# Silu and tanh gates in the input projections, and the delta rule's stream first in the scan, in a hybrid encoder block

## Chip, cores and metric

One kernel computes one encoder block on one core of a Trainium2 chip. The metric is the device time of a run in microseconds; lower is better. The engines are TensorE (PE in the rows; PEld are its weight loads), VectorE (DVE), ScalarE (ACT), GpSimd (POOL), and SyncE (SP), whose queue issues most DMAs.

## What is computed

All arrays are fp32, 512 tokens (T), width 2048 (D). Cut to what matters here:

```python
h = rmsnorm(x); proj = h @ w_in                        # columns: q k v z beta/alpha | Q F B I g
q, k, v = silu(short_conv(q, k, v)); q, k = l2norm(q), l2norm(k)
o_a = gdn_scan(q, k, v, fwd) + gdn_scan(..., bwd)      # gated delta rule, 8 heads
y_a = rmsnorm(o_a) * silu(z)
f = lb + (1 - lb) * sigmoid(F or B)                    # forget gates, one per direction
o_b = hgrn_scan(silu(Q), I, 1 - f, log f) both ways    # 8 heads
y_b = rmsnorm(o_b) * sigmoid(g)
x = x + concat(y_a, y_b) @ w_out
x = x + (silu(h2 @ w_gate) * (h2 @ w_up)) @ w_down     # h2 = rmsnorm(x)
out = rmsnorm(x)
```

The table of lower bounds `lb` comes from a softmax over two rows of logits.

## The kernel before

The kernel is one instruction stream that a scheduler of the language puts in order: it follows the order in which the Python code emits instructions, as a priority, and lets ready work go ahead by its own timing model. Each engine then runs its own list strictly in order, and so does each DMA queue.

Every large matrix product is done by `block_products`, in blocks of 256 output columns, with seven products for eight (a Strassen-like scheme, `PRODUCTS`), each operand split in a high and a low part (three matmuls each). All its matmuls stand in one line, L1022. Weights come by DMA as `raw` (SP queue) and are turned into `wsum` (VectorE, L974 to L976), `whr` and `whs` (high parts, ScalarE, L981 and L985), `wls` (low part, VectorE, L986) and `wlr` (low part; in the projections, the output projection and the down projection ScalarE writes the negative high part, L980, and a DMA issued by GpSimd adds `raw` to it, L982).

The stages, in order of the profile's time:

**Projections** (to about 842 us). `projections` walks the list `AHEAD` of 36 blocks: `k`, `q`, `v`, `z` of the delta rule, and `Q`, `F`, `B`, `I`, `g` of HGRN2, 0 to 3 each; the last two, `B3` and `g2`, are done together. After a block `combine` and L423 give `t`, 128 x 1024, and `post` finishes it and stores it to DRAM. `sigmoid` (L319 to L324) is exp(-x), ln(1 + .), exp(-.), three ACTIVATEs into the tile `sig`, of which there is one buffer. For `k`, `q`, `v` `conv_silu` first makes the five-tap convolution `acc`, then multiplies by the sigmoid on GpSimd (L338); `z` and `Q` are multiplied in L396, also on GpSimd; `F` and `B` take VectorE's L390 with `lb`, `g` takes the sigmoid as it is. `q` and `k` are normalised in the middle of the next block: two Ln (L355) and an Exp (L357 or L359). In the later blocks (`PREP`, indices 18 to 27) `gdn_head` prepares decay matrices for a head, with Abs and Exp on ScalarE (L478, L479) and multiplies on GpSimd (L477, L489), and `gdn_inverse` inverts 32 x 32 blocks on VectorE.

**Scan** (to about 1115 us). `gdn_blocks` and `gdn_pair` handle two heads of the delta rule, in four dependent steps forward and backward at once; `hgrn_pair` handles two heads of HGRN2, in seven levels that double the width, where VectorE multiplies X in place (L748, L750), ScalarE copies `kc` (L719) and TensorE multiplies (L722, L738), and then three dependent steps. Each pair ends in `finish` (L438 to L452): Square (L441), a sum over the partitions on TensorE (L445), two Ln (L446), an Exp (L447), two multiplies (L448, L451) and a store to `d_y`; its tiles have one buffer each. `merge` interleaves the streams: each generator yields a nominal duration, and the stream that is furthest behind emits next. PSUM is split: `psh` and `poh` for the HGRN pairs, `pss` and `pog` for the delta rule.

**Output projection** (`out_proj`). `Y_BLOCKS` gives the order in which the heads' outputs are loaded from `d_y` and used: 0 and 2 are the halves of the delta rule, 4 and 6 those of HGRN2. PSUM is now four pools of two banks, `ps0` to `ps3`, in the place of `psh`, `pss`, `poh`, `pog`; `Banks.take` gives the first column block pools 0 and 2, the next pools 1 and 3, and so on in turn. The first two column blocks are interleaved.

**FFN** (`gate_up`, `down`), with Silu in L1065.

The set of ScalarE's functions is asked for by name at the start (L88, the set that holds Ln and Exp) and near the end (L1105). In the profile one more load stands at L1065, in front of the first Silu, which the code doesn't ask for.

Of the kernel before, what the change touches and what calls it, by code (L numbers as in the profile page):

```python
# [9 lines left out]
F32 = mybir.dt.float32  # L10
# [7 lines left out]
P = 128  # L18
T = 512
# [51 lines left out]
class Block:  # L71
# [51 lines left out]
    def small_columns(self, pt, tmp):  # L123

        nc, a, const = self.nc, self.a, self.const
        lev = tmp.tile([P, 2, T], F32, name="sq", bufs=1).rearrange("p a t -> p (a t)")[:, :len(LEVELS) * 32]
        lev = lev.rearrange("p (l t) -> p l t", t=32)
        nc.sync.dma_start(out=lev, in_=a["c_lev"])
        self.tc.keep_in_program_order(nc.gpsimd.tensor_copy(out=self.lev, in_=lev))
        nc.sync.dma_start(out=self.tri, in_=a["c_tri"])  # L130
        self.tc.keep_in_program_order(nc.gpsimd.tensor_copy(out=self.trim, in_=self.tri))
        r1, r2 = self.r1, self.r2
        nc.tensor.transpose(out=pt[:, 0:120], in_=r1, identity=self.ident[0:120, 0:120])
        nc.tensor.transpose(out=pt[:, 128:178], in_=r2, identity=self.ident[0:50, 0:50])
        self.convw = const.tile([P, 5, 24], F32, name="convw")
        nc.vector.tensor_copy(out=self.convw.rearrange("p k c -> p (k c)"), in_=pt[:, 0:120])
        self.cols = const.tile([P, 50], F32, name="cols")
        nc.vector.tensor_copy(out=self.cols, in_=pt[:, 128:178])
        self.w2 = self.cols[:, 32:48]
        self.wga, self.whb = self.cols[:, 48:49], self.cols[:, 49:50]  # L140

        l0, l1 = self.cols[:, 0:16], self.cols[:, 16:32]
        m = tmp.tile([P, 16], F32, name="lbm")
        e = tmp.tile([P, 2, 16], F32, name="lbe")
        nc.vector.tensor_tensor(out=m, in0=l0, in1=l1, op=ALU.max)
        nc.vector.tensor_tensor(out=e[:, 0], in0=l0, in1=m, op=ALU.subtract)
        nc.vector.tensor_tensor(out=e[:, 1], in0=l1, in1=m, op=ALU.subtract)
        nc.scalar.activation(out=e, in_=e, func=AF.Exp)
        nc.vector.tensor_tensor(out=m, in0=e[:, 0], in1=e[:, 1], op=ALU.add)
        nc.vector.reciprocal(out=m, in_=m)  # L150
        self.lb = const.tile([P, 2, 16], F32, name="lb")
        nc.vector.tensor_tensor(out=self.lb[:, 0], in0=e[:, 0], in1=m, op=ALU.mult)
        nc.vector.tensor_scalar(out=self.lb[:, 1], in0=self.lb[:, 0], scalar1=-1.0, scalar2=1.0, op0=ALU.mult, op1=ALU.add)

# [157 lines left out]
    def projections(self, xops, chunk, tmp):  # L314
# [1 line left out]
        w = a["w_in"][0]  # L316
        ht = self.HT

        def sigmoid(src):  # L319
            s = tmp.tile([P, 2, T], F32, name="sig", bufs=1)  # L320
            nc.scalar.activation(out=s, in_=src, func=AF.Exp, scale=-1.0)
            nc.scalar.activation(out=s, in_=s, func=AF.Ln, bias=1.0)
            nc.scalar.activation(out=s, in_=s, func=AF.Exp, scale=-1.0)
            return s  # L324

        def conv_silu(t, ct):
            acc = tmp.tile([P, 2, T], F32, name="acc", bufs=2)
            for kk in range(2):
                w_ = lambda j: self.convw[:, j, ct + kk:ct + kk + 1]
                nc.scalar.activation(out=acc[:, kk], in_=t[:, kk], func=AF.Copy, scale=w_(2))  # L330
                for j in (0, 1, 3, 4):
                    sh = j - 2
                    o = slice(max(0, -sh), T - max(0, sh))
                    i = slice(max(0, sh), T - max(0, -sh))
                    nc.vector.scalar_tensor_tensor(out=acc[:, kk, o], in0=t[:, kk, i], scalar=w_(j), in1=acc[:, kk, o],
                                                   op0=ALU.mult, op1=ALU.add)
            s = sigmoid(acc)
            nc.gpsimd.tensor_tensor(out=acc, in0=acc, in1=s, op=ALU.mult)  # L338
            return acc

        def qk(t, col, dst, bias):
            acc = conv_silu(t, col // P)
# [34 lines left out]
        def post(kind, g, t):  # L377
            if kind == "k":
                return qk(t, OFF_K + g * 256, self.d_k[g], None)
            if kind == "q":  # L380
                return qk(t, OFF_Q + g * 256, self.d_q[g], self.qbias)
            if kind == "v":
                return tokens(conv_silu(t, (OFF_V + g * 256) // P), self.d_v[g])
            if kind == "I":
                return tokens(t, self.d_hv[g])
            s = sigmoid(t)
            if kind in "FB":
                for kk in range(2):
                    r = (kind == "B") * 8 + 2 * g + kk
                    nc.vector.tensor_scalar(out=s[:, kk], in0=s[:, kk], scalar1=self.lb[:, 1, r:r + 1],  # L390
                                            scalar2=self.lb[:, 0, r:r + 1], op0=ALU.mult, op1=ALU.add)
                dst = self.d_hf[(kind == "B") * 4 + g]
            elif kind == "g":
                dst = self.d_g[H // 2 + g]
            else:
                nc.gpsimd.tensor_tensor(out=s, in0=s, in1=t, op=ALU.mult)  # L396
                dst = (self.d_g if kind == "z" else self.d_hq)[g]
            nc.scalar.dma_start(out=dst.rearrange("h p t -> p h t"), in_=s)

# [441 lines left out]
    def scan(self):  # L841
        tc = self.tc
        with ExitStack() as st:
            pool = lambda name, **k: st.enter_context(tc.tile_pool(name=name, reuse_waits="tile", **{"bufs": 1, "side": "right", **k}))
            for n, b in (("psh", 2), ("pss", 2), ("poh", 1), ("pog", 1)):
                setattr(self, n, st.enter_context(tc.tile_pool(name=n, bufs=b, space=PSUM, reuse_waits="tile")))
            first, second, rest = pool("sca"), pool("scb"), pool("scc")
            self.sca = Pools(rest, hf=first, hq=first, C=first, X=second)
            self.sch, self.fin = pool("sch"), pool("fin")
            self.scb = pool("sc1"), pool("sc2", side="left")  # L850
            self.sc = pool("sc")
            self.gdn_ready = {}

            def gdn():
                yield from self.gdn_blocks(0)
                for i in range(0, H, 2):
                    yield from self.merge((0, self.gdn_pair(i)), *([(0, self.gdn_blocks(i + 2))] if i + 2 < H else []))

            def faster(i):
                for dt in self.hgrn_pair(i):  # L860
                    yield 0.75 * dt

            for _ in self.merge((0, faster(0), faster(4)), (40, faster(2), faster(6)), (40, gdn())):
                pass


    Y_BLOCKS = (0, 4, 6, 2)
    Y_SLOTS = (6, 7, 0, 1, 2, 3, 4, 5)

    def out_proj(self, late):  # L870
# [318 lines left out]
```

## Time and profile before

| | |
|---|---|
| time, median of 3 runs | 2677.78 us (2677.45 to 2679.18) |
| time of the profiled execution | 2677.02 us |
| its span, first to last instruction | 2675.2 us |
| mean granted TensorE clock | 0.968 of full speed |
| busy: TensorE, VectorE, ScalarE, GpSimd | 93%, 86%, 56%, 19% |

Shares of the whole span mix stages with different limits; the rows below are therefore taken by stretch. A row of instructions names line, engine, operation, output <- inputs with their shapes, and the count; "idle before" is time in which the engine waited, with what ended the wait.

### The profile page before, as it was taken

What the parts mean: (1) busy time and instruction counts of PE and PEld (TensorE: products, weight loads), DVE (VectorE), ACT (ScalarE), POOL (GpSimd) and SP (SyncE); (2) the same over time, 40 slices, a digit from 0 to 9 for tenths busy, and PEclk for the clock granted to TensorE, in tenths of its full rate; (3) what the DMA queues carried; (4) which work ended last, traced back from release to release, by engine and by line L of the source; (5) the groups of instructions that cost most, each with busy time, mean ns of one, the idle gap of its engine ahead of it and who ended that gap; (6) DMA issues with size and microseconds to landing.
All of it is one profiled execution on the core that took longest, in us unless ns stands there. A gap on an engine that the chain in (4) does not pass through costs nothing.

```text
span 2675.2 us, 55501 instructions
## 1 busy us (share of the span) xinstructions
PE 2489.8 (93%) x22511; PEld 2437.7 (91%) x22511; DVE 2298.1 (86%) x3598; ACT 1497.4 (56%) x2057; POOL 519.9 (19%) x400
## 2 busy tenths in 40 slices
PE   7999999989997788799999999999999989998996
PEld 6999999889986667799899999999999989998996
DVE  7989989998976876877988989889889888888885
ACT  7787777666665433656644444444444455655664
POOL 1233224443333532222000000000000012222221
PEclk9999999999998888999999999999999999999998
DMA  8889999999897443799343344333333388887875
GB/s 228 191 200 210 212 204 223 232 220 239 200 233 201 108 122 113 220 243 251 118 135 127 123 123 126 122 116 121 125 114 123 121 250 196 213 190 178 195 157 142
DMA packets 401708, 465.71 MB, mean 174 GB/s; under 512 B 48449, under 2 KB 354043, under 8 KB 401451
## 3 DMA queue, kind: packets, MB, share of 16 engines
q1 hardware_dynamic: 310939, 311.67, 38.3%
q0 software_dynamic: 71936, 103.83, 24.2%
q10 hardware_dynamic: 18576, 46.67, 5.0%
q8 instruction: 176, 2.88, 0.4%
q14 instruction: 81, 0.66, 0.1%
HBM read 303.66 MB, written 54.62 MB: 134 GB/s over the span
## 4 chain that ended last, share of the span: by engine, by line
PE 67%; DMA 10%; DVE 9%; issue 7%; ACT 4%; POOL 1%; SPq 1%; ACTq 0%; DVEq 0%; POOLq 0%
PE big L1022 64%; DMA wlr<-raw 4%; DMA raw<-in_w_out 1%; DVE X L750 1%; DVE wls L986 1%; DVE X L748 1%; DMA acc<-d_rows 1%; DMA tt<-d_t 1%; DMA raw<-in_w_down 1%; ACT wlr L980 1%; ACT whs L985 0%; ACT whr L981 0%; DVE wsum L975 0%; DMA sl<-d_l 0%; DVE wsum L974 0%
## 5 line engine op out<-in xcount | busy, mean ns | idle before, releaser
L985 ACT CAST whs<-wsum 128x1024 fp32r<-128x1024 f32 (+1 forms) x448 | 461.8, 1033 | 470.2 <-PE big L1022 242.4
L986 DVE TENSOR_TENSOR wls<-wsum,whs 128x1024 fp32r<-128x1024 f32 (+1 forms) x448 | 563.2, 1258 | 151.4 <-ACT whs L985 146.7
L982 POOL DMA_DIRECT2D wlr<-raw x272 | 323.7, 1190 | 1889.1 <-DVE tsum L941 893.8
L1022 PE MATMUL big<-oh,whs 128*128 128x256 f32 x2368 | 661.8, 283 | 3.7 <-ACT whs L985 3.7
L1022 PE MATMUL big<-ol,whs 128*128 128x256 f32 x2368 | 661.4, 282 | 0.0
L1022 PE MATMUL big<-oh,wls 128*128 128x256 f32 x2368 | 646.4, 283 | 3.3 <-DVE wls L986 3.3
L1022 PE MATMUL big<-oh,wlr 128*128 128x256 f32 x1776 | 493.4, 282 | 23.0 <-DMA wlr<-raw 22.8
L1022 PE MATMUL big<-oh,whr 128*128 128x256 f32 x1776 | 499.4, 283 | 13.2 <-ACT oh L956 9.8
L1022 PE MATMUL big<-ol,whr 128*128 128x256 f32 x1776 | 496.7, 281 | 0.6 <-DVE ol L958 0.6
L1022 PEld LDWEIGHTS big<-oh,whs 128*128 128x128 f32 x2368 | 449.9, 190 | 5.0 <-ACT whs L985 5.0
L1022 PEld LDWEIGHTS big<-ol,whs 128*128 128x128 f32 x2368 | 450.4, 190 | 0.0
L1022 PEld LDWEIGHTS big<-oh,wls 128*128 128x128 f32 x2368 | 443.3, 191 | 4.4 <-DVE wls L986 3.9
L1022 PEld LDWEIGHTS big<-oh,wlr 128*128 128x128 f32 x1776 | 332.9, 189 | 26.8 <-DMA wlr<-raw 26.5
L1022 PEld LDWEIGHTS big<-oh,whr 128*128 128x128 f32 x1776 | 335.7, 189 | 17.5 <-ACT oh L956 12.6
L974 DVE TENSOR_TENSOR wsum<-raw 128x512 f32<-128x512 f32 (+1 forms) x448 | 314.5, 703 | 42.0 <-DMA raw<-in_w_out 20.2
L1022 PEld LDWEIGHTS big<-ol,whr 128*128 128x128 f32 x1776 | 335.2, 189 | 1.9 <-DVE ol L958 1.7
L1022 PE MATMUL big<-tp,whs 128*128 128x256 f32 x1728 | 322.8, 283 | 2.7 <-ACT whs L985 2.7
L981 ACT CAST whr<-raw 128x768 fp32r<-128x768 f32 (+1 forms) x272 | 221.6, 815 | 157.2 <-PE big L1022 155.9
L1022 PEld LDWEIGHTS big<-tp,whs 128*128 128x128 f32 x1728 | 270.0, 192 | 3.9 <-ACT whs L985 3.1
L1022 PE MATMUL big<-tp,wls 128*128 128x256 f32 x864 | 242.7, 286 | 24.4 <-DVE wls L986 24.4
L980 ACT ACTIVATE wlr<-raw 128x768 fp32r<-128x768 f32 (+1 forms) x272 | 224.4, 825 | 58.9 <-DMA raw<-in_w_out 23.6
L985 ACT CAST whr<-raw 128x768 fp32r<-128x768 f32 x176 | 146.8, 835 | 159.0 <-PE big L1022 156.8
(319 smaller groups left out, 4699.4 us busy)
## 6 DMA issues: line engine op xcount, KB each, us to landing
wlr<-raw POOLq DMA_DIRECT2D x256, 384.0 KB, 5.9
raw<-in_w_in SPq DMA_DIRECT2D x144, 512.0 KB, 4.9
raw<-in_w_gate SPq DMA_DIRECT2D x88, 512.0 KB, 3.6
raw<-in_w_up SPq DMA_DIRECT2D x88, 512.0 KB, 3.6
raw<-in_w_down SPq DMA_DIRECT2D x80, 512.0 KB, 4.6
raw<-in_w_out SPq DMA_DIRECT2D x32, 512.0 KB, 5.9
d_t<-yt ACTq DMA_DIRECT2D x22, 512.0 KB, 2.9
tt<-d_t ACTq DMA_DIRECT2D x22, 512.0 KB, 4.5
```

The costliest lines, as they stand in the source:

```text
L748: nc.vector.tensor_tensor(out=xv[:, 0:2, n, 0, :], in0=xv[:, 0:2, n, 0, :], in1=tv[:, :, n, 1:2].broadcast_to([P, 2, nb // 2, hs]), op=ALU ...
L750: nc.vector.tensor_tensor(out=xv[:, 2:4, n, 1, :], in0=xv[:, 2:4, n, 1, :], in1=tv[:, :, n, 0:1].broadcast_to([P, 2, nb // 2, hs]), op=ALU ...
L974: tt(out=sm[:, :, 0:2], in0=raw[:, :, 0:1].broadcast_to([P, n, 2, P]), in1=raw[:, :, 1:3], op=ALU.add)
L980: nc.scalar.mul(out=lo, in_=src_, mul=-1.0)
L981: nc.scalar.copy(out=hi, in_=src_)
L982: nc.gpsimd.dma_start(out=lo.rearrange("p j x n -> p j (x n)").bitcast(F32), in_=src_.rearrange("p j x n -> p j (x n)"), accum_op=ALU.add)
L985: nc.scalar.copy(out=hi, in_=src_)
L986: tt(out=lo, in0=src_, in1=hi.bitcast(F32), op=ALU.subtract)
L1022: mm = lambda a, b, s, e: nc.tensor.matmul(prod[i], lhsT=a, rhs=b, start=s, stop=e, skip_group_check=True)
```

## The change

In `projections`, `sigmoid` is replaced by two helpers. `silu` is one ACTIVATE with Silu; it serves `k`, `q`, `v` (in place of three ACTIVATEs and the GpSimd multiply L338) and `z`, `Q` (in place of three and L396). `half_tanh` is one ACTIVATE, tanh(x / 2), for `F`, `B` and `g`; since sigmoid(x) = (1 + tanh(x / 2)) / 2, the two columns of `lb` that L390 uses become (1 - lb) / 2 and lb + (1 - lb) / 2, with one more small VectorE operation when they are made, and `g` gets an affine copy on ScalarE.

In `scan`, the delta rule's stream starts at 0 in place of 40 and with its durations times 0.8; the HGRN streams keep their starts and their factor 0.75. `Y_BLOCKS` becomes (0, 4, 2, 6).

```diff
-        nc.vector.tensor_scalar(out=self.lb[:, 1], in0=self.lb[:, 0], scalar1=-1.0, scalar2=1.0, op0=ALU.mult, op1=ALU.add)
+        nc.vector.tensor_scalar(out=self.lb[:, 1], in0=self.lb[:, 0], scalar1=-0.5, scalar2=0.5, op0=ALU.mult, op1=ALU.add)
+        nc.vector.tensor_tensor(out=self.lb[:, 0], in0=self.lb[:, 0], in1=self.lb[:, 1], op=ALU.add)
...
-        def sigmoid(src):
+        def silu(src, dst):
+            nc.scalar.activation(out=dst, in_=src, func=AF.Silu)
+            return dst
+
+        def half_tanh(src):
             s = tmp.tile([P, 2, T], F32, name="sig", bufs=1)
-            nc.scalar.activation(out=s, in_=src, func=AF.Exp, scale=-1.0)
-            nc.scalar.activation(out=s, in_=s, func=AF.Ln, bias=1.0)
-            nc.scalar.activation(out=s, in_=s, func=AF.Exp, scale=-1.0)
+            nc.scalar.activation(out=s, in_=src, func=AF.Tanh, scale=0.5)
             return s
...
-            s = sigmoid(acc)
-            nc.gpsimd.tensor_tensor(out=acc, in0=acc, in1=s, op=ALU.mult)
-            return acc
+            return silu(acc, acc)
...
-            s = sigmoid(t)
+            s = half_tanh(t) if kind in "FBg" else silu(t, tmp.tile([P, 2, T], F32, name="sig", bufs=1))
...
             elif kind == "g":
+                nc.scalar.activation(out=s, in_=s, func=AF.Copy, scale=0.5, bias=0.5)
                 dst = self.d_g[H // 2 + g]
             else:
-                nc.gpsimd.tensor_tensor(out=s, in0=s, in1=t, op=ALU.mult)
                 dst = (self.d_g if kind == "z" else self.d_hq)[g]
...
-            def faster(i):
-                for dt in self.hgrn_pair(i):
-                    yield 0.75 * dt
-
-            for _ in self.merge((0, faster(0), faster(4)), (40, faster(2), faster(6)), (40, gdn())):
+            def paced(steps, x):
+                for dt in steps:
+                    yield x * dt
+
+            hgrn = lambda i: paced(self.hgrn_pair(i), 0.75)
+            for _ in self.merge((0, paced(gdn(), 0.8)), (0, hgrn(0), hgrn(4)), (40, hgrn(2), hgrn(6))):
                 pass
-    Y_BLOCKS = (0, 4, 6, 2)
+    Y_BLOCKS = (0, 4, 2, 6)
```

## Rows read from the trace of the kernel before

**Rows 1.** Busy time by stretch: us, engines (instructions), granted clock, DMA share, GB/s

```profile
160.00:420.00 260.00, 259.92 (x2174) 258.67 (x2173) 235.68 (x344) 200.64 (x246) 78.93 (x58) 1.00 0.92 208
420.00:660.00 240.00, 220.48 (x1794) 217.77 (x1793) 226.59 (x332) 154.18 (x189) 101.84 (x65) 0.96 0.95 230
660.00:840.00 180.00, 170.42 (x1413) 168.99 (x1413) 145.38 (x238) 113.75 (x134) 56.28 (x41) 0.99 0.91 213
840.00:1070.00 230.00, 170.81 (x3465) 147.39 (x3465) 170.45 (x321) 94.22 (x164) 94.44 (x74) 0.84 0.43 128
...
1300.00:2160.00 860.00, 860.00 (x7242) 859.32 (x7242) 776.11 (x1129) 376.48 (x437) 2.40 (x2) 1.00 0.39 122
```

The engines stand in the order PE, PEld, DVE, ACT, POOL.

**Rows 2.** Waits of PE, 420 to 840: us in total, times, longest

```profile
PE big L1022 <- DVE wls L986: 23.8, 12, 5.4
...
PE big L1022 <- ACT whs L985: 0.7, 1, 0.7
```

**Rows 3.** Timeline of ACT, 838 to 858: start us, us, instruction

```profile
853.46 1.06 ACT L321 ACTIVATE sig<-t 128x1024 f32<-128x1024 f32 x1 [7.21 <-DMA d_hf<-sig]
...
856.60 0.66 ACT L719 COPY kc<-X 128x512 f32<-128x512 f32 x1
```

**Rows 4.** Line L794, the last matmuls of an HGRN pair

```profile
L794 PE MATMUL oT<-X,hS x96: 273/275/421, 903.0 to 1070.1; 128*128 128x128 f32 x96
```

**Rows 5.** Timeline of ACT, 900 to 1180: finishes in the scan

```profile
945.20 1.03 ACT L441 ACTIVATE sq<-oT 128x1024 f32<-128x1024 f32 x1
...
1071.24 1.00 ACT L441 ACTIVATE sq<-oT 128x1024 f32<-128x1024 f32 x1
...
1084.88 1.27 ACT L446 ACTIVATE sh<-sc,eps 128x512 f32<-128x512 f32 x2 [0.69 <-DMA d_y<-sh]
...
1115.16 1.02 ACT L441 ACTIVATE sq<-oT 128x1024 f32<-128x1024 f32 x1 [0.48 <-PE oT L632]
```

**Rows 6.** Timeline of DVE, 900 to 1180: L448 of two of those finishes

```profile
955.13 1.27 DVE L448 SCALAR_TENSOR_TENSOR sh<-oT,cols,sh 128x1024 f32<-128x1024 f32 x1
...
1088.27 1.28 DVE L448 SCALAR_TENSOR_TENSOR sh<-oT,cols,sh 128x1024 f32<-128x1024 f32 x1
```

**Rows 7.** Line L1022 by stretch: us, PE, PEld, clock, DMA share, GB/s

```profile
1070.00:1090.00 20.00, 0.98 (x6) 0.77 (x6) 0.91 1.06 285
1090.00:1130.00 40.00, 23.99 (x176) 22.16 (x177) 0.96 0.61 176
1130.00:1200.00 70.00, 64.12 (x533) 62.79 (x532) 1.00 0.99 252
```

**Rows 8.** Instruction groups of ACT, whole span: count, busy us, mean ns

```profile
L322 ACT ACTIVATE sig<-sig 128x1024 f32<-128x1024 f32 x32 | 33.8, 1055 | 0.3
...
L1065 ACT ACTIVATE yt<-yt 128x1024 f32<-128x1024 f32 x22 | 23.3, 1060 | 3.9 <-DVE yt L1062 3.9
```

**Rows 9.** Timeline of ACT around a table load

```profile
2657.53 0.25 ACT L1138 ACTIVATION_READ_ACCUMULATOR junk<-big 128x1 f32 x1
2657.80 1.28 ACT L1105 ACT_TABLE_LOAD   x1
2659.09 0.30 ACT L1108 ACTIVATE rf<-rf,eps 128x4 f32<-128x4 f32 x1
```

**Rows 10.** Instruction groups of POOL, 60 to 842

```profile
L338 POOL TENSOR_TENSOR acc<-acc,sig 128x1024 f32<-128x1024 f32 x12 | 34.6, 2884 | 19.5 <-ACT sig L323 19.5
...
L396 POOL TENSOR_TENSOR sig<-sig,t 128x1024 f32<-128x1024 f32 x8 | 21.0, 2622 | 11.8 <-ACT sig L323 10.4 <-DMA raw<-in_w_in 1.4
```

**Rows 11.** Instruction groups of DVE, 60 to 842

```profile
L986 DVE TENSOR_TENSOR wls<-wsum,whs 128x1024 fp32r<-128x1024 f32 x141 | 196.9, 1397 | 37.5 <-ACT whs L985 35.9 <-PE big L1022 0.9
```

**Rows 12.** Instruction groups of DVE, 1340 to 2100

```profile
L986 DVE TENSOR_TENSOR wls<-wsum,whs 128x1024 fp32r<-128x1024 f32 x154 | 188.0, 1223 | 59.4 <-ACT whs L985 56.5 <-PE big L1022 0.4
```

**Rows 13.** Instruction groups of DVE, 840 to 1115

```profile
L649 DVE SCALAR_TENSOR_TENSOR rr<-sc,ngam,vt 128x128 f32<-128x128 f32 x48 | 13.4, 342 | 5.2 <-PE sc L645 5.2
...
L665 DVE SCALAR_TENSOR_TENSOR S<-S,glast,sc 128x128 f32<-128x128 f32 x32 | 8.9, 340 | 1.7 <-PE sc L660 1.7
```

## The prediction

> **What bounds the kernel now.** I read the busy time by stretch first, then the waits of the engine that should be the bound, then the instruction lists of the two places where that engine is not busy. TensorE is the bound nearly everywhere: in 160 to 420 us of the projections and in 1300 to 2160 us of the FFN it is busy the whole time [rows 1], so nothing that ScalarE saves there can show. It has holes in three places that this change touches.
>
> First, the later projections: 19.5 us idle in 420 to 660 and 9.6 us in 660 to 840 [rows 1]. Of these 23.8 us are waits for VectorE's `wls` [rows 2], and VectorE is busy 226.6 of the 240 us of the first stretch [rows 1]: here VectorE is what is late, ScalarE is not (154 of 240).
>
> Second, the seam to the scan. The last two projection blocks share one buffer `sig`: the second gate waits 7.21 us for the store of the first, and behind it, in ScalarE's own order, stand the scan's first `kc` copies, which leave at 856.60 [rows 3].
>
> Third, the end of the scan. `hgrn_pair(6)` issues its last matmul at 1070.1 [rows 4], `gdn_pair(6)` goes on to 1115 [rows 5]. The output projection's first column block takes the PSUM banks of the HGRN streams (pools 0 and 2 of `Banks`, which lie where `psh` and `poh` lay), so it can't start before `finish` of `hgrn_pair(6)` has read them: its `Ln` ends at 1086.1 and its L448 at 1089.6 [rows 5, 6], and of the output projection's matmuls only 6 run before 1090 [rows 7]. In 1090 to 1130 it gets 176 matmuls through, where a full TensorE does 7242 in 860 us, 8.42 per us [rows 1, 7]: 20.9 us of work in 40, 19.1 us lost to the last GDN pair that is still running between them on the same queues. In 1130 to 1200 it does 533, 63.3 us of work in 70.
>
> **ScalarE's bill in the projections.** 32 gates of three ACTIVATEs of 1.055 us become 32 of one; Silu has a row, 1.060 us, Tanh has none and I take the same [rows 8]. Saved: 64 x 1.055 = 67.5 us. The four `g` gates get an affine copy, 4 x 1.06 = 4.2 us. Against that stand table loads. Today there are three in the program; one takes 1.28 us, begins 0.02 us after the operation ahead has ended, and the next operation begins 0.01 us after it [rows 9]. Silu after Ln and Exp needs one (L1065 has it), and after Silu every Ln or Exp needs one again. From the code: a `k` or `q` block gives Silu, then Ln twice and Exp (8 rounds); `gates_b` to `gates_d` give a few; eight `gdn_head`s give an Exp among the Silus of `v`, `Q` and `z`; each of eight `finish`es in the scan gives Ln, Ln, Exp; `token_scale` gives Ln, Exp. No row shows which set the compiler takes for an Ln after Silu when nothing asks for one by name (L88 and L1105 do). If it holds Exp too: 16 + 3 + 8 + 1 + 0 = 28 loads. If Ln and Exp come from two sets: 24 + 6 + 16 + 16 + 2 = 64. I take 62, the dear end: 46 in the projections, 59.0 us. ScalarE's net there is -67.5 + 4.2 + 59.0 = -4.3 us, nothing; with 28 loads it would be some -29 us. Neither moves TensorE in 160 to 420, where ScalarE is busy 200.6 of 260 us and waits for buffers.
>
> The Trainium skill (ScalarE: Activation LUTs, section What ACT_TABLE_LOAD costs) gives a switch 2.66 us, a load of 1.283 us and a drain of 1.38 us. The row agrees on the load and shows no drain beside it; by the page, 62 loads would be 165 us of ScalarE and its net in the projections +59 us.
>
> **What VectorE gains.** 12 multiplies of 2.88 us and 8 of 2.62 us leave GpSimd [rows 10]. While GpSimd works VectorE is slow: the same `wls` subtraction takes 1397 ns in the projections and 1223 ns in the FFN, where GpSimd is idle [rows 11, 12], 12.5% of the former. On VectorE's 372 us in 420 to 840 that is 46 us. Of GpSimd's 158 us there [rows 1] the 12 multiplies that fall into that time (four `v`, eight `Q` and `z`) are 12 x 2.66 = 32 us, a fifth: 9 us less for VectorE. TensorE's wait for it is 23.8 us, so the bounds are 0 and -24; I take **-7 us**. If the cover (spare ScalarE time) is gone because loads come in bursts behind a `gdn_head`, the term turns to +6: eight heads then cost two loads each, 20.5 us, less the 2.1 us that each of some seven gates between them gives back.
>
> **The seam.** The chain is gate, L390, store, gate, `kc`. The first gate loses two ACTIVATEs, 2.1 us; the second (`g2`) loses two and gets a copy, 1.0 us. L390 and the store stay. **-3 us**, bounds 0 and -4. The one more VectorE operation on `lb`, 16 columns wide, is below 0.3 us and early: 0.
>
> **The scan's order.** `merge` puts instructions in order; its times decide rank alone. In `merge`'s units a GDN pair is 38, an HGRN pair 99 x 0.75 = 74. Before: HGRN streams end at 148 and 188, GDN at 40 + 18 + 4 x 38 = 210. After: GDN ends at 0.8 x 170 = 136, and the stream of `hgrn_pair(6)`, unchanged at 188, is last. `Y_BLOCKS` follows: GDN's second half is now third, HGRN's second half last. So the last GDN pair goes ahead of HGRN's end, and what it did to the output projection's front ends. But the start of that front is HGRN's end, and that moves:
> - the last GDN pair's VectorE work, 12 L649 of 0.342 and 8 L665 of 0.340 [rows 13], and, as an estimate from L448's 1.28 [rows 6], four operations of that size and a half one for `kt`, finish and the first copy: 4.1 + 2.7 + 5.8 = 12.6 us, which at the scan's own rate (170.5 busy of 230) takes 17 us: +17;
> - 16 table loads, 20.5 us of ScalarE, which is busy 94 of 230: bounds 0 and +20.5, I take +4, since what sits behind a finish mostly waits for VectorE;
> - GDN in front, with the longest chain of short steps, fills part of VectorE's 59.5 idle us: bounds 0 and -25, I take -10;
> - `finish` of `hgrn_pair(6)` lay 18.3 us from 1071.24 to 1089.55, since its tile `sh` waited for the store of a GDN finish. One that nobody holds up takes 945.20 to 956.4, 11.2 us [rows 5, 6], with two loads 13.8: -4.5.
>
> Sum +6.5: the front starts at 1097 in place of 1090. It then runs at the full rate: of the 19.1 + 6.7 us lost I give back 19 and leave the rest to the weights' transfers. Net **-12.5 us**. DMA issues in the scan are the same in number; those of GDN now stand ahead of HGRN's on SP, up to 1 us each, inside the bound of the third item.
>
> Sum: -7 - 3 - 12.5 = -22.5 on the profiled execution's 2677.0; the median of the runs is 0.8 above it. I predict **2655**.
>
> **Rivals.**
> 1. *The scan's end only changes hands.* HGRN's end takes the place of GDN's, 1115, since one HGRN pair alone has no partner to fill its waits, and nothing of the output projection can fill them (its first banks are HGRN's). The front starts at 1129; by then the old one had done 20 us of work, of which 2 come back: +18, with -10 from the rest 2685. It decides against the change from an HGRN end of about 1107 on. For it: an HGRN pair is the longest unit; against: at 1070 the old order had only 12 us of VectorE's scan work left. Chance 0.20.
> 2. *The loads sit on the path.* No relief in the projections (0 in place of -7), and all 16 scan loads in the chain (+20.5 in place of +4): -22.5 + 7 + 16.5 = +1, 2678. For it: every finish is a chain; against: in 420 to 840 TensorE waits 0.7 us for ScalarE's `whs` [rows 2]. Chance 0.13. The Trainium skill (same page, section Table sets: the hidden batching unit) says to batch by set, against this change; by its 2.66 us this case would give some 22 us more.
> 3. *Nothing arrives.* The front is fed by transfers (DMA share 0.99 in 1130 to 1200 [rows 7]) and the projections' holes are elsewhere: 2675. Chance 0.07.
>
> **How the numbers follow.** The forecast has 0.60, its own range 2634 to 2670. A difference of 0.2%, 5 us, is about what a measurement of this kernel can tell. Faster: the 0.60, and a third of rival 2: 0.65. Slower: most of rival 1 and a third of 2: 0.23. Same: 0.12. The range takes in rival 1: 2632 to 2689; the low end is all of the projections' holes or all of the fill.
>
> **What would show it.** Right: L338 and L396 gone; L986 in the projections under 1350 ns and TensorE's wait for it under 18 us; some 60 loads of 1.28 us; `kc` leaving about 3 us earlier; all four GDN finishes ahead of the last HGRN one; output-projection matmuls at 8 per us from their start. Wrong: a start past 1107, loads fewer than 30, or TensorE waiting for ScalarE in the projections.

## The result and the profile after

The changed kernel takes 2717.95 us (median of 4 runs, 2715.22 to 2725.37), the kernel before in the same session 2678.48 (2677.45 to 2685.65). The ratio is 1.0143, with a 95% interval of [1.0122, 1.0164]: by the ratio 38 us slower, where 2655 was forecast and 2689 was the far end of the range. The profiled execution of after took 2715.22 us, its span is 2713.4.

Line numbers of after are 3 or 4 higher than those of before (L1022 is L1026, L986 is L990, L794 is L797, L446 is L449, L972 is L976, L892 is L896).

I read the stretches first (us; PE, PEld, DVE, ACT, POOL busy; granted clock; DMA share; GB/s), which answer to [rows 1].

```profile
420.00:660.00 240.00, 214.58 (x1711) 210.81 (x1710) 196.78 (x321) 150.99 (x182) 89.50 (x54) 0.95 0.90 220
660.00:840.00 180.00, 173.66 (x1448) 172.88 (x1447) 138.93 (x244) 104.72 (x124) 48.62 (x41) 0.99 0.98 229
840.00:1070.00 230.00, 167.94 (x3106) 145.26 (x3105) 155.42 (x294) 94.07 (x150) 102.72 (x72) 0.83 0.43 129
1070.00:1130.00 60.00, 40.97 (x566) 33.71 (x564) 37.04 (x73) 32.75 (x46) 6.93 (x7) 0.84 0.31 91
1130.00:1200.00 70.00, 57.54 (x402) 55.24 (x403) 57.41 (x95) 40.21 (x57) 11.55 (x10) 0.85 0.80 206
```

VectorE lost 29.8 us of work in 420 to 660 (226.59 before), and TensorE still did less there (220.48 before). In 1070 to 1130 the transfers are down to a DMA share of 0.31, where the kernel before has this row:

```profile
1070.00:1130.00 60.00, 47.59 (x338) 43.31 (x337) 53.88 (x95) 37.93 (x54) 11.91 (x8) 0.94 0.76 212
```

In before that stretch holds the out-projection's first weights and inputs. In after the first weights are not asked for before 1107.45 and the first inputs not before 1120.41 (the rows of SyncE's queue below). The waits of PE in 420 to 840, of after, answer to [rows 2]; the group of `wls` on DVE in 60 to 842 answers to [rows 11].

```profile
PE big L1026 <- DVE wls L990: 20.0, 11, 4.7
PE big L1026 <- ACT whs L989: 6.4, 3, 4.6
PE big L1026 <- DMA wlr<-raw: 5.0, 5, 2.6
```

```profile
L990 DVE TENSOR_TENSOR wls<-wsum,whs 128x1024 fp32r<-128x1024 f32 x140 | 180.5, 1291 | 60.6 <-ACT whs L989 60.2
```

The `wls` subtraction is faster, 1291 ns for 1397, and VectorE now waits 60.2 us for ScalarE's `whs` (35.9 before). TensorE waits 6.4 us for that `whs` itself, 0.7 before. ScalarE's timeline at the seam answers to [rows 3]:

```profile
846.95 1.06 ACT L328 ACTIVATE sig<-t 128x1024 f32<-128x1024 f32 x1 [7.82 <-DVE t L426]
...
857.57 1.06 ACT L328 ACTIVATE sig<-t 128x1024 f32<-128x1024 f32 x1 [3.76 <-DMA d_hf<-sig]
...
860.19 1.26 ACT L722 COPY kc<-X 128x512 f32<-128x512 f32 x2 [0.47 <-ACT sig L397]
```

From gate to gate it is 10.6 us instead of 14.2 (839.29 to 853.46 before), but the first of them comes 7.7 us later, and `kc` leaves at 860.19 instead of 856.60.

The scan's end, first the last matmuls of an HGRN pair [rows 4] and of a GDN pair, then ScalarE's finishes [rows 5]:

```profile
L797 PE MATMUL oT<-X,hS x96: 275/275/377, 930.0 to 1120.1; 128*128 128x128 f32 x96
...
L635 PE MATMUL oT<-L,w x128: 274/275/421, 889.9 to 1081.1; 128*128 128x128 f32 x128
```

```profile
1095.99 1.28 ACT L449 ACT_TABLE_LOAD   x1 [0.38 <-DMA d_y<-sh]
1097.29 1.26 ACT L449 ACTIVATE sh<-sc,eps 128x512 f32<-128x512 f32 x2
1098.57 1.28 ACT L450 ACT_TABLE_LOAD   x1
1099.86 1.06 ACT L450 ACTIVATE sh<-sh 128x1024 f32<-128x1024 f32 x1
...
1120.37 1.02 ACT L444 ACTIVATE sq<-oT 128x1024 f32<-128x1024 f32 x1 [5.48 <-PE oT L797]
```

HGRN's end went from 1070.1 to 1120.1 and GDN's from 1115 to 1081: they changed places. Each finish has two table loads, one for Ln and one for Exp. The same time on SyncE's queue and on PE, of after:

```profile
1105.89 1.47 SPq L453 DMA_DIRECT2D gt<-d_g  x1
1107.45 1.53 SPq L976 DMA_DIRECT2D raw<-in_w_out  x3
1120.41 0.88 SPq L896 DMA_DIRECT2D yt<-d_y  x2
```

```profile
1121.45 1.98 PE L448 MATMUL sc<-sq,ones 128*128 128x512 f32 x4 [1.11 <-ACT sq L444]
1132.74 0.58 PE L1026 MATMUL big<-oh,whr 128*128 128x256 f32 x1 [9.30 <-ACT oh L960]
```

The two first `yt` loads, the inputs of the out-projection, leave 0.3 us behind HGRN's last matmul, though the half that they fetch (heads 0 to 3 of GDN) began its last finish at 973.36. The profile's list of waits names the matmul:

```profile
SPq L896 <- PE oT L797: 11.4, 1, 11.4
```

The kernel before has the same picture 50 us earlier (`yt` at 1070.47, HGRN's last matmul at 1070.1):

```profile
1065.85 4.07 SPq L972 DMA_DIRECT2D raw<-in_w_out  x3
1070.47 1.83 SPq L892 DMA_DIRECT2D yt<-d_y  x2
```

So the out-projection gets no input before HGRN ends, and in after only HGRN's own last finish of the scan is left to run beside its start. Of its matmuls none runs before 1130 (182 in before [rows 7]); the first comes at 1132.74, in before at 1085.62:

```profile
1085.62 0.39 PE L1022 MATMUL big<-oh,whr 128*128 128x256 f32 x1
```

The weights have a wait of their own: ahead of them in SyncE's order stand stores of the scan's finishes, which wait for VectorE's last product, once for 32.0 us in after (26.5 in before):

```profile
SPq L455 <- DVE sh L454: 62.8, 4, 32.0
```

### The profile page after: what moved, and what is told of

It reads as the page before. It is cut to its first block, busy times and chain, and to the rows that moved or that the text cites. A ratio compares the mean times of both kernels' runs of the same rounds, so it can differ in the third digit from the quotient of the medians.

```text
span 2713.4 us, 55500 instructions
## 1 busy us (share of the span) xinstructions
PE 2501.3 (92%) x22511; PEld 2445.7 (90%) x22511; DVE 2251.1 (83%) x3599; ACT 1510.4 (56%) x2051; POOL 485.3 (18%) x380
## 4 chain that ended last, share of the span: by engine, by line
PE 46%; DMA 7%; DVE 4%; issue 4%; ACT 2%; POOL 0%; ACTq 0%; POOLq 0%; DVEq 0%; SPq 0%
PE big L1026 43%; DMA wlr<-raw 4%; DMA raw<-in_w_down 1%; DMA raw<-in_w_out 1%; DVE ol L962 1%; DVE wls L990 0%; PE oT L635 0%; DVE wsum L978 0%; ACT wlr L984 0%; PE oT L774 0%; ACT oh L960 0%; PE sc L656 0%; PE sc L725 0%; DVE tsum L945 0%; DMA d_y<-sh 0%
## 5 line engine op out<-in xcount | busy, mean ns | idle before, releaser
L990 DVE TENSOR_TENSOR wls<-wsum,whs 128x1024 fp32r<-128x1024 f32 (+1 forms) x448 | 548.4, 1225 | 178.7 <-ACT whs L989 172.2
L986 POOL DMA_DIRECT2D wlr<-raw x272 | 323.3, 1190 | 1962.4 <-ACT wlr L984 968.1
L1026 PE MATMUL big<-oh,whs 128*128 128x256 f32 x2368 | 659.7, 282 | 1.2 <-ACT whs L989 1.2
L1026 PE MATMUL big<-ol,whs 128*128 128x256 f32 x2368 | 659.9, 281 | 0.0
L1026 PE MATMUL big<-oh,wls 128*128 128x256 f32 x2368 | 645.4, 282 | 3.8 <-DVE wls L990 3.8
L1026 PE MATMUL big<-oh,whr 128*128 128x256 f32 x1776 | 501.9, 284 | 26.6 <-ACT oh L960 20.5
L1026 PE MATMUL big<-oh,wlr 128*128 128x256 f32 x1776 | 496.7, 283 | 27.4 <-DMA wlr<-raw 27.4
L1026 PE MATMUL big<-ol,whr 128*128 128x256 f32 x1776 | 498.6, 282 | 0.7 <-DVE ol L962 0.7
L1026 PEld LDWEIGHTS big<-oh,whs 128*128 128x128 f32 x2368 | 449.3, 190 | 1.8 <-ACT whs L989 1.8
L1026 PEld LDWEIGHTS big<-ol,whs 128*128 128x128 f32 x2368 | 449.8, 190 | 0.0
L1026 PEld LDWEIGHTS big<-oh,wls 128*128 128x128 f32 x2368 | 442.5, 191 | 4.7 <-DVE wls L990 4.2
L1026 PEld LDWEIGHTS big<-oh,whr 128*128 128x128 f32 x1776 | 337.6, 191 | 32.1 <-ACT oh L960 24.8
L1026 PEld LDWEIGHTS big<-oh,wlr 128*128 128x128 f32 x1776 | 335.6, 190 | 31.3 <-DMA wlr<-raw 30.9
L978 DVE TENSOR_TENSOR wsum<-raw 128x512 f32<-128x512 f32 (+1 forms) x448 | 308.5, 689 | 46.9 <-DMA raw<-in_w_in 20.1
L1026 PEld LDWEIGHTS big<-ol,whr 128*128 128x128 f32 x1776 | 337.7, 190 | 1.8 <-DVE ol L962 1.7
L1026 PE MATMUL big<-tp,whs 128*128 128x256 f32 x1728 | 323.3, 283 | 6.7 <-ACT whs L989 6.7
L1026 PEld LDWEIGHTS big<-tp,whs 128*128 128x128 f32 x1728 | 269.8, 192 | 7.7 <-ACT whs L989 7.7
L1026 PE MATMUL big<-tp,wls 128*128 128x256 f32 x864 | 243.3, 285 | 21.6 <-DVE wls L990 21.6
```

What stands on the lines that cost most here:

```text
L978: tt(out=sm[:, :, 0:2], in0=raw[:, :, 0:1].broadcast_to([P, n, 2, P]), in1=raw[:, :, 1:3], op=ALU.add)
L986: nc.gpsimd.dma_start(out=lo.rearrange("p j x n -> p j (x n)").bitcast(F32), in_=src_.rearrange("p j x n -> p j (x n)"), accum_op=ALU.add)
L990: tt(out=lo, in0=src_, in1=hi.bitcast(F32), op=ALU.subtract)
L1026: mm = lambda a, b, s, e: nc.tensor.matmul(prod[i], lhsT=a, rhs=b, start=s, stop=e, skip_group_check=True)
```

## The experiments

Theory 1: the loss sits at the scan's end, which changed hands. Theory 2: the table loads cost it. The table takes three times of each profiled execution (us: last matmul of HGRN, last of GDN, first Silu of the FFN) beside the ratio of the timed runs to before. "Tail" is the time from the later of the two ends to that Silu. From that Silu to the end every kernel takes another 1337 to 1348 us.

| kernel | HGRN | GDN | Silu | tail | ratio, 95% interval |
|---|---|---|---|---|---|
| before | 1070.1 | 1114.8 | 1337.0 | 222.2 | |
| after | 1120.1 | 1081.1 | 1378.2 | 258.1 | 1.0143 [1.0122, 1.0164] |
| e1 gates alone | 1070.5 | 1117.2 | 1347.2 | 230.0 | 1.0013 [1.0000, 1.0027] |
| e2 order alone | 1104.9 | 1068.3 | 1363.9 | 259.0 | 1.0109 [1.0082, 1.0135] |
| e3 after, no switches | 1107.5 | 1071.1 | 1360.4 | 252.9 | 1.0094 [1.0071, 1.0116] |
| e4 after, banks exchanged | 1119.6 | 1080.6 | 1376.5 | 256.9 | 1.0147 [1.0125, 1.0168] |
| e5 after, other memory | 1123.2 | 1082.2 | 1377.3 | 254.1 | 1.0161 [1.0144, 1.0178] |
| e6 block order alone | 1070.9 | 1115.8 | 1348.4 | 232.6 | 1.0033 [1.0021, 1.0045] |
| e7 GDN from 20 | 1098.6 | 1097.2 | 1355.4 | 256.8 | 1.0081 [1.0066, 1.0096] |
| e8 gates, one table | 1060.7 | 1103.7 | 1330.2 | 226.5 | 0.9990 [0.9977, 1.0004] |
| e9 HGRN ahead | 1045.4 | 1124.7 | 1354.4 | 229.7 | 1.0073 [1.0054, 1.0093] |
| e10 gates, no switches | 1051.7 | 1097.3 | 1320.9 | 223.6 | 0.9966 [0.9951, 0.9981] |
| e12 after, one table | 1113.9 | 1076.9 | 1370.2 | 256.3 | 1.0108 [1.0090, 1.0126] |
| e13 e8 with GDN from 36 | 1068.1 | 1116.4 | 1341.7 | 225.3 | 1.0028 [1.0014, 1.0041] |
| e14 after, old block order | 1114.9 | 1077.2 | 1369.5 | 254.6 | 1.0142 [1.0125, 1.0159] |
| e16 late gates, one table | 1056.4 | 1098.9 | 1330.1 | 231.2 | 0.9969 [0.9956, 0.9983] |
| e17 e8 again | 1062.2 | 1105.2 | 1330.0 | 224.8 | 0.9979 [0.9967, 0.9992] |

**The two halves of the change (e1, e2).** e1 is after with the lines of the scan's order and `Y_BLOCKS` of before; e2 is before with these of after:

```
-            for _ in self.merge((0, faster(0), faster(4)), (40, faster(2), faster(6)), (40, gdn())):
+            for _ in self.merge((0, paced(gdn(), 0.8)), (0, hgrn(0), hgrn(4)), (40, hgrn(2), hgrn(6))):
...
-    Y_BLOCKS = (0, 4, 6, 2)
+    Y_BLOCKS = (0, 4, 2, 6)
```

> The gates by Silu and tanh alone, with the scan's order and the out-projection's block order of before. Theory 1 (the time is lost at the scan's end, which changes hands to the lower-bound recurrence, and the out-projection waits for that recurrence's PSUM banks): this kernel stands near before, 2670 to 2686 us (-7 from VectorE's relief, at most +8 from the seam being late as in the changed kernel's trace). Theory 2 (the table loads cost it): it takes most of the +38, 2700 us or more, and the loads number 50 or more.

> The scan's order and the out-projection's block order alone, with the sigmoid of three activations. Table loads stay at 3. Theory 1: the lower-bound recurrence's last matmul moves from 1070 to about 1110 to 1120, the out-projection's first matmul comes near 1130, and the kernel takes 2705 to 2715 us. Theory 2: the order is worth what was forecast for it or nothing, 2665 to 2680 us.

e1 came out at 2686.84 us, 0.13% over before with an interval that touches 1, and 0.8 us past the upper end that theory 1 gave; e2 at 2708.47, 1.09% over. The order is the larger part, about 29 of the 38 us, as theory 1 said. e2 has 3 table loads, as before, and the same end as after: HGRN last, and the first `yt` right behind it.

```profile
L794 PE MATMUL oT<-X,hS x96: 275/275/421, 920.9 to 1104.9; 128*128 128x128 f32 x96
```

```profile
1093.57 1.52 SPq L973 DMA_DIRECT2D raw<-in_w_out  x3
1105.24 0.88 SPq L893 DMA_DIRECT2D yt<-d_y  x2
```

**Switches and banks (e3, e4).**

```
-            nc.scalar.activation(out=dst, in_=src, func=AF.Silu)
+            nc.scalar.activation(out=dst, in_=src, func=AF.Copy)
...
-            nc.scalar.activation(out=s, in_=src, func=AF.Tanh, scale=0.5)
+            nc.scalar.activation(out=s, in_=src, func=AF.Copy, scale=0.0625)
```

> The changed kernel with a copy in place of each Silu and a scaled copy in place of each tanh of the projections: it leaves out the nonlinearity of the gates, and all engines' instruction counts stay, but no table has to be changed before the tail, neither in the projections nor in the finishes. Theory 1: the scan's end stays at the lower-bound recurrence and the time comes down only by what the seam was late, to 2700 to 2712 us. Theory 2: most of the loss goes with the loads, 2670 to 2685 us.

```
-        self.ps = Banks([... for i in range(4)], ((0, 2), (1, 3)))
+        self.ps = Banks([... for i in range(4)], ((1, 3), (0, 2)))
```

> The changed kernel with the out-projection's two pairs of PSUM pools exchanged, so that its first column block takes the banks of the delta rule, which ends at 1081 us, and the second those of the lower-bound recurrence, which ends at 1120. Theory 1 with the banks as what holds it: the out-projection's first matmuls start near 1090 to 1100 instead of 1131, and 15 to 30 us come back, 2688 to 2703 us. Theory 1 with the tail's own length as what holds it (the last blocks of the input are late anyway): 2710 to 2718 us. Theory 2: no change, 2718 us.

e3 took 2704.63 us, within what theory 1 gave: some 13 us of the 38 belong to the switches. e4 took 2719.73, no change: the PSUM banks of HGRN, which the prediction named, are not what holds the out-projection's start. Its first `yt` still left 0.3 us behind HGRN's last matmul (1119.94 and 1119.6).

**The balance (e7, e9).** Each is before with the scan's plan changed, here in short:

```
 e7: (0, hgrn(0), hgrn(4)), (40, hgrn(2), hgrn(6)), (20, gdn())      hgrn at 0.75
 e9: (0, hgrn(0), hgrn(4)), (30, hgrn(2), hgrn(6)), (40, gdn())      hgrn at 0.5
```

> The kernel before with one number changed: the delta rule's stream starts at 20 in the scan's plan instead of 40, so that in the plan both recurrences end together; the out-projection's block order and the sigmoid stay. Theory 1, as the first four runs leave it (the out-projection's first loads of the recurrences' outputs wait for the lower-bound recurrence's last matmul, whose place in memory they take, and from there some 210 us of out-projection follow whatever runs beside it): the lower-bound recurrence ends between 1070 and 1105, near 1090, the first load follows it within 1 us, and the kernel is as much later, about 2700 us (2692 to 2708). Rival: the loss of the order came from the order of the out-projection's blocks, which is that of before here: 2676 to 2686 us.

> The kernel before with the lower-bound recurrence moved the other way: its steps are planned at 0.5 of their cost instead of 0.75, its second stream from 30 instead of 40, the delta rule unchanged. Theory 1 in its plain form (time follows the end of the lower-bound recurrence): that end comes 10 to 25 us before 1070, the out-projection's first load with it, and the kernel takes 2655 to 2672 us. Rival: below some point the delta rule's end (1115 in the kernel before) holds the out-projection's last two blocks, and its tail, with less beside it, gives the gain back: 2676 to 2690 us.

e7 landed at 2700.75, as theory 1 has it, and with the old block order. e9 is a miss: HGRN ended at 1045.4, 25 us earlier, and the kernel was slower, 2699.66. GDN's end went out to 1124.7, and with GDN last it is that end which counts. The out-projection's first matmul came at 1056.05, 79 us passed between the two ends (45 in before), and the tail was not shorter for it. The plain form "time follows HGRN's end" fell. What holds is in the table's tail column: when GDN ends last the tail is 222 to 233 us, when HGRN ends last (or both together) it is 253 to 259. The end of the scan as a whole, whichever recurrence it is, plus one of two tails, gives the time of the first Silu.

**Where the out-projection's inputs lie (e5).** The scan's pools are made in another order, GDN's first, and `io` is made ahead of `wst`:

```
-            first, second, rest = pool("sca"), pool("scb"), pool("scc")
...
+            self.sc = pool("sc")
+            self.scb = pool("sc1"), pool("sc2", side="left")
+            self.fin = pool("fin")
+            first, second, rest = pool("sca"), pool("scb"), pool("scc")
```

> The changed kernel with its on-chip memory laid out otherwise: the scan takes the delta rule's tiles first, and the out-projection's input tiles come ahead of its weight tiles, so that the input tiles fall on the delta rule's memory (free near 1081 us in the changed kernel) and the weights and operands on that of the lower-bound recurrence. If it is the place in memory that holds the first loads of the recurrences' outputs at the end of the lower-bound recurrence, these loads leave SyncE's queue 20 to 50 us ahead of that end instead of 0.3 us behind it. The time then tells what else waits there: if the weights and operands wait for the same end, as their place says, 2708 to 2718 us; if only the inputs did, 2690 to 2705 us. If the loads stay 0.3 us behind that end, memory was not the reason.

The first `yt` loads moved to GDN's end, 1082.27 (GDN's last matmul started at 1082.2), so it is the place in memory that they wait for. The weights now went later, to 1133.14, behind the last stores of the scan, and the time did not improve: 2725.20, past both ranges.

```profile
1082.27 0.88 SPq L897 DMA_DIRECT2D yt<-d_y  x2
1133.14 2.14 SPq L977 DMA_DIRECT2D raw<-in_w_out  x3
```

So freeing the inputs gives nothing while the weights come later. ScalarE's first `oh`, made from these inputs, started at 1129.94, and the first matmul at 1139.44, behind a wait for the weights' `whr`. Whether operands and weights wait for HGRN's memory as the inputs did, or for their place in the queues' order behind the scan's last finish, was not tried apart.

**The block order (e6, e14).** e6 is before with `Y_BLOCKS` of after, e14 after with that of before.

> The kernel before with the out-projection's block order of after alone: the lower-bound recurrence's second half comes last instead of the delta rule's. Theory: with the delta rule still ending last (1115 us), its second half is now wanted one place earlier, and the time stays or grows a little, 2678 to 2688 us. Rival: the block order is part of the loss of the scan's new order, 2690 us or more.

> The changed kernel with the out-projection's block order of before, in which the delta rule's second half comes last. In the changed kernel the lower-bound recurrence ends last, so the old order wants its second half one place earlier. If the block order was chosen rightly for the new scan order and only the scan order loses: 2718 to 2728 us. If the new block order is itself part of the loss, as the 9 us of its run alone may say: 2705 to 2712 us.

e6 lost 0.33%, 9 us, more than the first theory allowed; its tail is 10 us longer than that of before. That the half that is finished last is wanted one place earlier is the likely reason. e14 took 2718.79, as much as after: under the new scan order the block order neither costs nor gives. It is no part of the loss, and the rival's reading of e6 falls.

**The loads in the scan (e8, e12, e17).** One line at the head of the scan; e8 and e17 are e1 with it, e12 is after with it:

```
+            self.tc.keep_in_program_order(self.nc.scalar.preload_act_table_set("natural_log_exp_and_others"))
```

> The gates alone (scan and block order of before), with one table that holds both Ln and Exp loaded at the start of the scan, so that the 16 table loads of the finishes and the two of the token scale go, and those of the projections stay. Theory of the loads: the finishes' loads stand on the path of the last finish (each finish is about 2.6 us longer): 2680 to 2685 us beside 2687 of the gates alone. Rival: the loads of the scan are all hidden: 2686 to 2688 us.

> The changed kernel with one table that holds both Ln and Exp loaded at the start of the scan, so that the 16 loads of the finishes and the two of the token scale go. With the gates alone the same edit gave 10 us. If those loads stand on the path whatever the order, 2704 to 2712 us; if they cost only where the delta rule ends last, 2715 to 2719 us.

> The gates alone with one table from the start of the scan on, once more: 2676 us again, some 4 us under before, if its first result holds, and a few us above the kernel with the late gates alone if the loads of the projections cost what the other runs say.

The loads of the program fall from 57 to 40. e8 took 2676.47 us, more of a gain than was expected, and e17 2675.63, by their ratios 6 to 9 us below e1; e12 took 2710.99, 9 us below after. The loads of the finishes are on the path in either order. The finish of the last HGRN pair in e1 and in e8:

```profile
1085.38 1.28 ACT L449 ACT_TABLE_LOAD   x1
1086.67 1.27 ACT L449 ACTIVATE sh<-sc,eps 128x512 f32<-128x512 f32 x2
1087.95 1.28 ACT L450 ACT_TABLE_LOAD   x1
1089.25 1.06 ACT L450 ACTIVATE sh<-sh 128x1024 f32<-128x1024 f32 x1
```

```profile
1075.50 1.27 ACT L449 ACTIVATE sh<-sc,eps 128x512 f32<-128x512 f32 x2 [0.23 <-DMA d_y<-sh]
1076.80 1.06 ACT L450 ACTIVATE sh<-sh 128x1024 f32<-128x1024 f32 x1
```

**The gates without any switch (e10)** is e1 with the edit of e3.

> The gates alone (scan and block order of before), with a copy in place of each Silu and a scaled copy in place of each tanh of the projections, which leaves out the nonlinearity of the gates and with it every table switch before the tail. Theory of the loads (the switches of the projections eat what VectorE and GpSimd gain): the projections end about 14 us earlier than with the gates and the kernel takes 2668 to 2675 us. Rival: the loads are hidden beside TensorE and the difference between the two kernels with the scan's order of after came from elsewhere: 2683 to 2688 us.

2672.27 us, 0.34% under before. The last gate of the projections comes at 843.8, 10 us ahead of before (853.46; 848.8 to 850.9 in the four other kernels with the sigmoid throughout) and 9 ahead of e8 (852.8); of these 9 the timed runs keep 3.5 to 6.4 (0.9979 and 0.9990 against 0.9966). PE's waits of e10 in 420 to 840 show part of what the switches had done:

```profile
PE big L1025 <- DVE wls L989: 21.6, 12, 4.8
PE big L1025 <- ACT whs L988: 1.7, 1, 1.7
```

TensorE's wait for `whs` is back at 1.7 (6.4 in after), that for the transfer of the weights at 0.2 (5.0). VectorE's own wait for `whs` in 60 to 842 is not: 61.9 us without a switch, 60.2 in after. It is time that VectorE has to spare, and the switches did not make it.

**Two attempts at a better version (e13, e16).** e13 is e8 with GDN's stream from 36 instead of 40. e16 keeps the order of before and the sigmoid for the early gates, and has the one-table line:

```
-            s = sigmoid(t)
+            if kind in "Qz":
+                s = tmp.tile([P, 2, T], F32, name="sig", bufs=1)
+                nc.scalar.activation(out=s, in_=t, func=AF.Silu)
+            elif (kind, g) in (("g", 0), ("g", 2), ("g", 3), ("F", 3), ("B", 3)):
+                s = tmp.tile([P, 2, T], F32, name="sig", bufs=1)
+                nc.scalar.activation(out=s, in_=t, func=AF.Tanh, scale=0.5)
+                nc.scalar.activation(out=s, in_=s, func=AF.Copy, scale=0.5, bias=0.5)
+            else:
+                s = sigmoid(t)
```

> The gates, the scan and block order of before, the one table at the start of the scan, and the delta rule's stream from 36 in the plan instead of 40. In the runs so far the token scale comes about 247 us after the end of the lower-bound recurrence where that ends last, and about 215 us after the delta rule's last finish where that is last, whichever is later; the two meet where the finish is some 32 us behind, and with the start at 40 it is 43 behind. If these two ends are all that counts, 36 gains 1 to 4 us: 2672 to 2676 us. If the balance of before is already the best one, as the kernels with 20 and with the faster lower-bound recurrence lie 20 us above it, 2677 to 2685 us.

> The scan and block order of before, Silu and tanh only for those gates of the projections that come behind the last Ln of the key and query norms (all of Q and z, three of the four g, the last F and B: 13 of the 24 gated blocks), the sigmoid of before for the rest, and one table for Ln and Exp loaded at the start of the scan: 6 loads ahead of the scan's end instead of 52 in the gates alone, and 16 of the 32 activations of the new gates' blocks and 8 multiplications on GpSimd go. Theory of the loads: the relief of VectorE arrives in part and the scan is untouched, 2668 to 2677 us. Rival: without the early gates nothing is gained, 2678 to 2684 us.

e13 missed: 2687.17. It lies past both ranges: with four units less in the plan the end of the scan came 12.7 us later than in e8, which the two-ends rule can't foresee; why is open. e16 took 2673.34 us, 0.9969 [0.9956, 0.9983], with 9 table loads in all: it beats both kernels. (Its expectation miscounts: it is 13 of 32 blocks, which lose 26 activations, and five get a copy.) With 13 new blocks for 32, and 6 new loads for 54, it ends 8 us under before; e17 lies within its interval.

## Why the prediction was wrong, by its steps

**The step that failed: "Sum +6.5: the front starts at 1097 in place of 1090."** In e2, which has no new table load, the out-projection's first matmul came at 1114.88 instead of 1085.62, 29.3 us later, where the three items without the loads (+17, -10, -4.5) gave +2.5; HGRN's end moved by 34.8. In after that end moved by 50, and the first matmul came at 1132.74, 47 us later. The item that was mis-sized is the first one. It priced the last GDN pair by VectorE's busy time, 12.6 us, stretched to 17. But what stood behind HGRN's end was not an amount of work; it was 44.7 us of a chain (1070.1 to 1114.8), in whose waits the out-projection started. Moved ahead, it cost that time less what a better packed scan gave back: in e2 the scan as a whole ended at 1104.9 instead of 1114.8. That 9.9 us is near the item "-10 for GDN in front", but no run prices that item by itself.

**"It then runs at the full rate ... I give back 19"** failed with it. From its first matmul to the FFN's first Silu the out-projection takes 251.4 us in before, 249.0 in e2 and 245.5 in after: 2 to 6 us came back, not 19. So the last GDN pair had cost it little, or as much was lost again at the uncovered start. The out-projection's start needs inputs, operands and weights that come one behind the other, and in before this went on during GDN's last 45 us. Without that cover the tail is 258.1 us instead of 222.2, 36 us longer; in e2 259.0. In 1130 to 1200 the matmuls are 402 (533 before), and TensorE waits for `oh` first (the row at 1132.74). For e2 the sum at the FFN's first Silu (1363.9 against 1337.0) is -9.9 for the scan's end and +36.8 for the tail, +26.9 us, and the timed difference is 29. That it is the cover which the change took away is the reading that fits all these runs; which of the three supplies sets the length of the uncovered start is open.

**Rival 1 was the right mechanism** ("HGRN's end takes GDN's place 1115", the front at 1129): measured 1120.1 and 1132.7. Its price was too low, 2685, because it took the gates' 10 us as a gain in hand and had 20 us of the old front's work as all that the late start could cost. That its two times were met so closely in after is in part luck: in e2 HGRN ended at 1104.9, ahead of the 1107 from which the rival decides against the change, the first matmul came at 1114.88, and 29 us were lost all the same. Its reason, the PSUM banks, is refuted by e4 as what holds the start; for the inputs the trace and e5 put SBUF memory in their place.

**"16 table loads ... I take +4"**, with bounds of 0 and +20.5. e12 says 9 us in the new order (1.0108 against 1.0143), e1 against e8 and e17 6 to 9 us in the old one. The cause given, that what sits behind a finish waits for VectorE, leaves out ScalarE's own order: in after the last finish's two loads stand ahead of the cast of `oh` there, and TensorE's wait for `oh` in front of its first out-projection matmul is 9.30 us, where e12 has 6.62:

```profile
1123.91 0.80 PE L1027 MATMUL big<-oh,whr 128*128 128x256 f32 x2 [6.62 <-ACT oh L961]
```

These 2.7 us are the time of two loads; the rest of the 9 is not traced to single finishes.

**"ScalarE's bill ... nothing"** was near in its sum and wrong in its reading. 54 new loads came where 62 were expected, each 1.283 us, and Ln and Exp did take one each; in 60 to 842 ScalarE is busy 536.1 us in after and 546.4 in before. The Trainium skill (ScalarE: Activation LUTs, section Table sets: the hidden batching unit) has Ln followed by Exp at one load, from a set that holds both. In after each of the eight finishes shows two, until the set is asked for by name (e8). The bill in sum is a saving, but its loads fall where something waits: TensorE's wait for `whs` grew from 0.7 to 6.4 us although ScalarE did less, and without the switches it is 1.7 (e10). Gates with all loads reach the last gate at 852.8 to 857.6 in nine kernels (after, e1, e4, e5, e8, e12, e13, e14, e17), those without at 843.4 and 843.8 (e3, e10).

**"-7 us" for VectorE and "-3" at the seam**: their sum fits a kernel without the switches, as e10 is 0.34% below before, 9 us, with 10 forecast. The split is not shown: in e10 TensorE's wait for `wls` is 21.6 us, only 2.2 below that of before. The seam itself gave 3.5 us in after. The marks that the prediction set for them: `wls` at 1291 ns (under 1350 said), TensorE's wait for it 20.0 (under 18 said), `kc` 3.6 us later and not earlier. With the loads the two terms are gone and e1 stands at +3.5 us, from 0 to 7 by its interval. Two of the signs of being wrong showed as well: a start past 1107, and TensorE waiting for ScalarE.

The sum of the two halves alone is 3.5 + 29 = 33, of both together 38; the 5 us between them lie within the intervals.

## What to carry to other kernels

When a piece of work is moved from the end of a stage to its middle, price it by the time during which it stood alone at the end, and ask what was running in its gaps: that work loses its cover. Which stream ends last decides what the next stage can start on; look at whose memory the next stage's first tiles take before changing that. Cheaper activation functions paid here where they were grouped by table (e16, 8 us), and a named table for Ln and Exp behind Silu and tanh gave 6 to 9 us for one line.

## What was not expected of the hardware

TensorE's granted clock was low at the uncovered start. The out-projection's line L1026 alone, in after (us; PE, PEld busy; granted clock; DMA share; GB/s):

```profile
1130.00:1140.00 10.00, 4.09 (x16) 3.50 (x17) 0.61 1.02 265
1140.00:1150.00 10.00, 9.82 (x55) 9.32 (x56) 0.66 0.81 257
1150.00:1160.00 10.00, 10.00 (x87) 10.00 (x86) 1.00 0.96 235
```

Its line L1022 at its start in before:

```profile
1080.00:1090.00 10.00, 0.98 (x6) 0.77 (x6) 0.85 1.10 259
1090.00:1100.00 10.00, 4.11 (x23) 3.51 (x24) 0.84 0.78 263
```

In after the engine had been idle for 9.3 us ahead of it; in before it ran the last GDN pair's matmuls in between. At 0.61 and 0.66, nearer the lower of the two levels of 1.2 and 2.4 GHz, it did 55 matmuls in a stretch in which it was 9.82 us busy, and 87 in the next at 1.00. In before the first two stretches ran at 0.85 and 0.84. As an estimate from these rows, the 71 matmuls of the first two stretches of after, 13.9 us busy, would have taken 8.2 us at the rate of the third: the clock has a part of some 6 us in the loss, and no run takes it out by itself.
